# Whole loads of x, five fills ahead of the latents, and PSUM banks handed out by readiness, in a two-layer hybrid decoder trunk

## The chip, the cores and the metric

The kernel runs on one core of a Trainium2 chip. The metric is the device time of one execution in microseconds (us). In the rows below PE is the matrix engine (TensorE), DVE the vector engine, ACT the scalar engine, POOL GpSimd and SP the engine that here only issues DMAs. PEclk is the clock that TensorE was granted, 1.00 being the higher of its two levels (2.4 GHz) and 0.50 the lower (1.2 GHz).

## The reference

Two layers over x of 512 tokens by 1024 channels, float32. The part of a layer that the change touches:

```python
c_act = jax.nn.silu(c)
mod = c_act @ w_ada[l] + b_ada[l]
sh1, sc1, gt1, sh2, sc2, gt2 = [m[:, None, :] for m in jnp.split(mod, N_MOD, axis=-1)]
h = rms_norm(x, g_norm1[l]) * (1.0 + sc1) + sh1
u = h @ w_in[l] + b_in[l]
q_lat, kv_lat, k_rope, q_sb, k_sb, v_sb, gate_mla, gate_sb = jnp.split(u, IN_SPLIT_POINTS, axis=-1)
...
y_mla = causal_softmax_attention(q, k, v_mla)
y_sb = stick_breaking_attention(...)
merged = (jax.nn.sigmoid(gate_mla) * (y_mla @ w_branch_mla[l])
          + jax.nn.sigmoid(gate_sb) * (y_sb @ w_branch_sb[l]))
x = x + gt1 * (merged @ w_out[l])
```

q, k and the two latents are RMS-normed, and q and k get a rotary embedding from positions. A second norm and a gated MLP with a causal convolution of width 3 follow in each layer.

## The kernel before

Channels lie on the 128 partitions and the 512 tokens on the free axis, so x is eight tiles `xs[0..7]` of 128x512. Every float32 operand of a large product is split into a high and a low part, and one product is three matmuls (`mm3`): the high part of a weight is made by a cast on ACT or DVE (out of a buffer of the tag "raw", of which there are three), the low part by a subtraction on DVE.

The program is recorded as a list of operations. A list scheduler (`order`) then puts them into one order for each engine by estimated costs and by a priority, which is the place in the program plus `R.bias`; the lowest goes first, so that work with a bias of 400 stands back behind 400 later operations and slips into gaps. All engines' instructions therefore carry the one line that emits them, L1240 (L1235 for a table load of ACT). A buffer of the tag "ps", one of PSUM's eight banks, is granted in program order.

Layer 0 begins so. SP issues sixteen loads of 128x256, first the left halves of all eight tiles of x, then the right halves. ACT squares a half tile at a time, DVE adds the squares, and one matmul with a matrix of ones gives the sum over all channels of that half (`rsqrt_wide`). ACT issues four small loads of the positions and one of the rotary frequencies, between its squares. DVE works out rotary angles (`rope_tables`) on 128x512.

The modulation (sc1 and sh1, a column of 128 for each of the eight channel tiles k) is made in two ways. `ada_products` does it on PE: four loads of weights and 16 products of 128x1, which are 32 rows in the trace. `ada_tile` does it on DVE: two loads of 256 KB of `wada` and two multiply-and-sum instructions of 128x512 (CUSTOM_DVE in the rows). Before the change k = 0 and k = 1 take `ada_products`, k = 2 to 7 take `ada_tile`, two of them for each k.

The first projection of layer 0 fills eight banks, that is eight column blocks of 128 of w_in: four of the latents and the shared rotary key, four of the stick-breaking heads. It loops over k, and each k adds three matmuls to each bank, 24 matmuls in all. For k = 0 the work is in two halves of 256 tokens with seven banks; the eighth bank is done whole at k = 1. Then come `latents` (norms of the latents on ACT and DVE with small products in between), and a weave of the latent attention, the stick-breaking attention and *fills*: a fill is one more column block of the first projection, either a part of a stick-breaking head (`sb_proj`) or a gate (`gate`), 24 matmuls of 128x512 that need nothing but h and a weight. `FILLS` of them stand in the program ahead of the latents, at bias 400. `GATES` is how many of the 16 gates are fills at all; the others are done behind the attention. Layer 1 has the same shape, with seven banks.

Of the kernel before, what the change touches and what calls it, by code (L numbers as in the profile page):

```python
# [40 lines left out]
UNITS = 241  # L41
# [40 lines left out]
class Slot:  # L82
    def __init__(self, tag, dt, n):
        self.tag, self.dt, self.n = tag, dt, n
        self.mem = None
        self.log = []
        self.users = []
        self.index = 0
# [6 lines left out]
class Program:  # L95
# [3 lines left out]
    AFTER = {"pe": 200.0, "act": 145.0, "dve": 130.0, "pool": 160.0, "dma": 1050.0, "adma": 1050.0}  # L99
# [39 lines left out]
    def order(self):  # L139
# [8 lines left out]
        for o in self.ops:  # L148
            for t in o.slots:
                if t.users[0] is o or self.tags[t.tag]["bufs"]:  # L150
                    waiting.setdefault(t, []).append(o)
                    o.left += 1
# [14 lines left out]

        def release(o, time):
            o.left -= 1
            if o.left == 0:  # L170
                push(time, o)

        def grant(tg, time):
            while tg["next"] < len(tg["queue"]) and tg["used"] < tg["bufs"]:
# [26 lines left out]
        for o in self.ops:  # L201
            if o.left == 0:
                push(0.0, o)
        for tg in self.tags.values():
            grant(tg, 0.0)
        done = []
        while events:
# [6 lines left out]
            elif kind == "end":  # L214
# [7 lines left out]
                for q in o.succ:  # L222
                    lat = 0.0 if (q.eng == "pe" and o.eng == "pe") else self.AFTER[o.eng] + (80.0 if q.eng == "pe" else 0.0)
                    q.left -= 1
                    if q.left == 0:
                        push(time + lat, q)
            for name, e in engines.items():
# [82 lines left out]
FILLS = 2  # L310
EVERY = 4
GATES = 4
BIAS_E = 100
BIAS_R = 150
# [20 lines left out]
def trunk_kernel(ctx, tc, keys, xT, wstream, wada, cols, cvec, pos, freqs, out):  # L335
# [8 lines left out]
    def bank():  # L344
        return R.slot("ps")
# [64 lines left out]
    def dma(o, i, nbytes, writes=(), reads=(), eng="dma"):  # L410
        R.add(eng, "dma_start", max(nbytes / 360.0 + 10, 480.0), None, writes, reads, out=o, in_=i)
# [22 lines left out]
    HALF = (slice(0, S // 2), slice(S // 2, S))  # L434
    colt = [const(NCOL) for _ in range(DEPTH)]
    load(colt[0], cols[0], "adma")
    row = R.slot("raw", D)[0:1]
    load(row, cvec, "adma")
    xs = [slot() for _ in range(KC)]

    def load_x(n):
        for k in range(KC):
            load(xs[k][:, HALF[n]], xT[k][:, HALF[n]])

    load_x(0)
# [3 lines left out]
    act(row, row, AF.Silu)  # L449
# [11 lines left out]
    R.bias = BIAS_S  # L461
    for n in range(2):
# [4 lines left out]
        act(cact[:, c], ps, AF.Copy, alone=True)  # L467
    R.bias = 0
# [61 lines left out]
    def rsqrt_wide(sq, div, out=None):  # L530

        ps = bank()[:, 0:sq.n]
        mm(ps, ones, sq, True, True)
        r, q = (slot() if out is None else out)[:, 0:sq.n], slot()[:, 0:sq.n]
# [5 lines left out]
        return r  # L540
# [13 lines left out]


# [120 lines left out]
    def rope_tables():  # L676

        posv, freq = slot(dt=I32), slot()[:, 0:1]
        for i in range(4):
            load(posv[:, i * P:i * P + P], pos[32 * i:32 * i + 1].to_broadcast([P, P]), "adma")  # L680
        load(freq, freqs, "adma")
        sign = epsc[:, 3:4]
        for i in range(4):
            memset(sign[32 * i:32 * i + 32], -1.0 if i % 2 else 1.0)
        a, k = slot(), slot()
        R.add("dve", "tensor_copy", 330.0, None, [a], [posv], out=a, in_=posv)
# [13 lines left out]
        act(cosr, k, AF.Sin, scale=-1.0, bias=epsc[:, 2:3])  # L700
        act(sinr, a, AF.Sin, scale=sign)
# [276 lines left out]
    def layer(l, xs, xsrc, first, r=None, later=None):  # L978
# [3 lines left out]
        if l == 0:  # L982

            acc = [slot()[:, 0:S // 2] for _ in HALF]

            def start_norm(n):
                for k in range(KC):
                    x = xs[k][:, HALF[n]]
                    if k == 0:
                        act(acc[n], x, AF.Square)  # L990
                    else:
                        sq = slot()[:, 0:S // 2]
                        act(sq, x, AF.Square)
# [9 lines left out]
            load_x(1)  # L1003
            R.bias = BIAS_R
            rope_tables()
            R.bias = 0
# [328 lines left out]
```

## Time and profile before

| what | value |
|---|---|
| time, three runs | 1470.82 to 1473.1 us, median 1471.37 |
| the profiled execution | 1474.78 us, span 1473.0 us |
| mean granted clock of TensorE | 0.993 |
| busy: PE, DVE, ACT | 1445.1, 1029.7, 675.6 us |

The span runs from the first to the last instruction of the profiled execution; its time has 1.8 us more. A busy time sums what the trace counts as work on that engine; a matmul that runs at the lower clock, or drags, counts as busy all the same.

### The profile page before, as it was taken

The page shows a single profiled execution, that of the slowest core. Times are in us where ns is not written, and L with a number is a line of the kernel's source. Part 1 is how long each engine was busy: PE and PEld are TensorE (multiplying, and loading weights), DVE is VectorE, ACT ScalarE, POOL GpSimd, SP SyncE. Part 2 cuts the span into 40 slices and gives each one's busy share as a digit, 9 for nine tenths or more (in the row PEclk, how much of TensorE's full clock was granted, in tenths as well). Part 3 has the DMA queues.
Part 4 walks back from the last instruction along what each step waited for, and adds up shares of the span by engine and source line. Part 5 has one row for each costly group of instructions (what it writes and reads, how often), then busy time and mean ns, then how long its engine had stood idle before and what let it go on. Part 6 is the DMA issues. An engine that isn't in the chain of part 4 may idle for free.

```text
span 1473.0 us, 19263 instructions
## 1 busy us (share of the span) xinstructions
PE 1445.1 (98%) x7121; PEld 1218.4 (83%) x7121; DVE 1029.7 (70%) x2069; ACT 675.6 (46%) x1224; POOL 3.3 (0%) x18
## 2 busy tenths in 40 slices
PE   5999999999999999999999999999999999999998
PEld 4877888888988888888898788888889888888887
DVE  5888899956699987878364888944639675356641
ACT  4377876433444422334144787933416342233420
POOL 0000000000000000000000000000000000000000
PEclk9999999999999999999999999999999999999999
DMA  8421138755266676534230112433603333322311
GB/s 289 154 61 47 58 95 300 250 193 191 73 212 194 208 236 222 164 122 127 98 95 16 56 47 74 127 102 90 198 13 115 115 90 124 87 85 88 113 44 43
DMA packets 69792, 184.80 MB, mean 125 GB/s; under 512 B 7873, under 2 KB 11201, under 8 KB 69698
## 3 DMA queue, kind: packets, MB, share of 16 engines
q1 hardware_dynamic: 68832, 183.15, 39.2%
q8 instruction: 56, 0.92, 0.3%
q10 hardware_dynamic: 866, 0.41, 0.2%
q14 instruction: 38, 0.31, 0.1%
HBM read 179.34 MB, written 4.19 MB: 125 GB/s over the span
## 4 chain that ended last, share of the span: by engine, by line
PE 92%; ACT 3%; DVE 2%; DMA 1%; issue 0%; SPq 0%; DVEq 0%; ACTq 0%
PE ps L1240 92%; ACT s L1240 3%; DVE s L1240 2%; DMA s<-in_xT_dram 1%; DMA s<-in_wada_dram 0%; DMA s<-in_freqs_dram 0%; DMA raw<-in_wstream_dram 0%; DVE sm L1240 0%; SPq L1240 0%; ACT sm L1240 0%; DVEq L1323 0%; DVE c L1240 0%; DVEq L1240 0%; ACTq L1240 0%
## 5 line engine op out<-in xcount | busy, mean ns | idle before, releaser
L1240 PE MATMUL ps<-s,s 128*128 128x512 f32 (+2 forms) x6625 | 1413.2, 372 | 5.5 <-DVE s L1240 2.4
L1240 PEld LDWEIGHTS ps<-s,s 128*128 128x128 f32 x6625 | 1157.8, 190 | 220.0 <-DVE s L1240 6.9
L1240 ACT ACTIVATE s<-raw 128x512 fp32r<-128x512 f32 (+1 forms) x413 | 247.1, 622 | 364.5 <-PE ps L1240 207.9
L1240 DVE TENSOR_TENSOR s<-raw,s 128x512 fp32r<-128x512 f32 (+1 forms) x470 | 308.3, 682 | 151.1 <-PE ps L1240 86.3
L1240 ACT ACTIVATE s<-s 128x512 f32<-128x512 f32 (+7 forms) x372 | 210.9, 585 | 225.4 <-DVE s L1240 216.0
L1240 DVE SCALAR_TENSOR_TENSOR s<-ps,c,s 128x510 f32<-128x510 f32 (+4 forms) x249 | 175.3, 727 | 108.9 <-PE ps L1240 104.1
L1240 DVE TENSOR_TENSOR s<-s,s 128x512 fp32r<-128x512 f32 (+6 forms) x318 | 194.4, 621 | 31.7 <-ACT s L1240 23.9
L1240 ACT ACTIVATE s<-ps,c 128x512 f32<-128x512 f32 (+2 forms) x141 | 98.7, 721 | 80.4 <-PE ps L1240 80.1
L1240 DVE CUSTOM_DVE_ANT_0 s<-s,c,c 128x512 f32<-128x512 f32 x92 | 68.2, 747 | 15.1 <-DMA s<-in_wada_dram 15.0
L1240 DVE CUSTOM_DVE_ANT_0 s<-s,c,sm 128x512 f32<-128x512 f32 x92 | 68.3, 749 | 12.4 <-DMA s<-in_wada_dram 9.6
L1240 ACT ACTIVATE s<-ps 128x512 f32<-128x512 f32 (+3 forms) x118 | 63.5, 549 | 21.4 <-PE ps L1240 20.4
L1240 PE MATMUL ps<-c,s 128*128 128x1 f32 (+1 forms) x264 | 53.9, 264 | 3.2 <-DVE s L1240 2.4
L1240 PE MATMUL ps<-s,c 128*128 128x256 f32 (+3 forms) x140 | 48.3, 380 | 4.9 <-DVE s L1240 4.3
L1240 DVE TENSOR_SCALAR s<-ps,c 128x512 f32<-128x512 f32 (+1 forms) x33 | 25.9, 786 | 34.8 <-PE ps L1240 32.5
L1240 DVE TENSOR_SCALAR s<-raw 128x512 fp32r<-128x512 f32 (+1 forms) x57 | 23.7, 420 | 35.0 <-PE ps L1240 29.3
L1240 PEld LDWEIGHTS ps<-c,s 128*128 128x128 f32 x264 | 41.6, 193 | 7.0 <-DVE s L1240 3.9
L1240 ACT ACTIVATE s<-s,c 128x256 fp32r<-128x256 f32 (+1 forms) x56 | 27.5, 525 | 30.6 <-DVE s L1240 30.5
L1240 DVE SCALAR_TENSOR_TENSOR s<-s,c,s 128x256 fp32r<-128x256 f32 (+3 forms) x72 | 37.9, 554 | 0.6 <-ACT s L1240 0.4
L1240 PEld LDWEIGHTS ps<-s,c 128*128 128x128 f32 x140 | 26.3, 196 | 10.7 <-DVE s L1240 5.9
L1240 DVE TENSOR_TENSOR s<-ps,s 128x512 fp32r<-128x512 f32 (+1 forms) x40 | 25.0, 633 | 4.3 <-ACT s L1240 3.9
L1240 DVE TENSOR_TENSOR s<-s,ps 128x512 f32<-128x512 f32 x32 | 21.4, 683 | 6.4 <-PE ps L1240 6.4
L1240 DVE SCALAR_TENSOR_TENSOR s<-ps,s 128x512 f32<-128x512 f32 (+1 forms) x38 | 23.2, 614 | 2.5 <-ACT s L1240 2.2
(50 smaller groups left out, 251.9 us busy)
## 6 DMA issues: line engine op xcount, KB each, us to landing
raw<-in_wstream_dram SPq DMA_DIRECT2D x221, 512.0 KB, 3.7
s<-in_wada_dram SPq DMA_DIRECT2D x184, 256.0 KB, 4.0
raw<-in_wstream_dram SPq DMA_DIRECT2D x12, 448.0 KB, 3.4
s<-in_xT_dram SPq DMA_DIRECT2D x16, 128.0 KB, 4.0
s<-in_wstream_dram SPq DMA_DIRECT2D x8, 256.0 KB, 5.2
s<-in_xT_dram SPq DMA_DIRECT2D x8, 256.0 KB, 3.4
keep<-s SPq DMA_DIRECT2D x8, 256.0 KB, 2.7
s<-keep SPq DMA_DIRECT2D x8, 256.0 KB, 4.0
```

The lines of the kernel that those rows point to most:

```text
L1240: getattr(engines[o.eng], o.name)(**kw)
```

## The change

1. The start. x comes in eight whole loads of 128x512. Squares are whole, except that of the last tile, which is in halves, as are the two matmuls with ones and what follows from them. Positions and frequencies are loaded by SP behind x, as 128x128; ACT issues none of these loads. The rotary tables are worked out on 128x128, and 32 ACT copies of 32x128 spread them.
2. Only k = 0 takes `ada_products`; k = 1 is on DVE as the others. For k = 0 all eight banks are in halves.
3. `FILLS` goes from 2 to 5 and `GATES` from 4 to 8, in both layers.
4. The scheduler: a PSUM bank is granted when the first product into it could run, the most urgent first, and some of its costs are changed (the delay of a DMA 1050 to 2000).

```diff
-    AFTER = {"pe": 200.0, "act": 145.0, "dve": 130.0, "pool": 160.0, "dma": 1050.0, "adma": 1050.0}
+    AFTER = {"pe": 200.0, "act": 145.0, "dve": 130.0, "pool": 160.0, "dma": 2000.0, "adma": 2600.0}
...
+            elif wants(o):
+                heapq.heappush(wanting, (o.prio, o.seq, o))
+                banks(time)
+
+        def banks(time):
+            tg = self.tags["ps"]
+            while wanting and tg["used"] < tg["bufs"]:
+                o = heapq.heappop(wanting)[2]
+                t = next(t for t in o.slots if self.tags[t.tag]["psum"])
+                tg["used"] += 1
+                t.index = tg["free"].pop(0)
+                release(o, time)
...
-FILLS = 2
+FILLS = 5
 EVERY = 4
-GATES = 4
+GATES = 8
 BIAS_E = 100
-BIAS_R = 150
+BIAS_R = 250
+BIAS_T = 20
 BIAS_S = 60
 BIAS_A = 40
 BIAS_F = 400
...
     row = R.slot("raw", D)[0:1]
     load(row, cvec, "adma")
+    act(row, row, AF.Silu)
+    load(colt[0], cols[0], "adma")
     xs = [slot() for _ in range(KC)]
-
-    def load_x(n):
-        for k in range(KC):
-            load(xs[k][:, HALF[n]], xT[k][:, HALF[n]])
-
-    load_x(0)
+    for k in range(KC):
+        load(xs[k], xT[k])
+    posv, freq = slot(dt=I32)[:, :P], slot()[:, 0:1]
+    load(posv, pos)
+    load(freq, freqs)
     cact = const(D)
     ccol = const(KC)
     act(ccol, colt[0][:, C_C:C_C + KC], AF.Silu)
-    act(row, row, AF.Silu)
```

```diff
@@ -675,15 +706,8 @@
 
     def rope_tables():
 
-        posv, freq = slot(dt=I32), slot()[:, 0:1]
-        for i in range(4):
-            load(posv[:, i * P:i * P + P], pos[32 * i:32 * i + 1].to_broadcast([P, P]), "adma")
-        load(freq, freqs, "adma")
-        sign = epsc[:, 3:4]
-        for i in range(4):
-            memset(sign[32 * i:32 * i + 32], -1.0 if i % 2 else 1.0)
-        a, k = slot(), slot()
-        R.add("dve", "tensor_copy", 330.0, None, [a], [posv], out=a, in_=posv)
+        a, k = slot()[:, :P], slot()[:, :P]
+        R.add("dve", "tensor_copy", 130.0, None, [a], [posv], out=a, in_=posv)
         ts(a, a, freq, ALU.mult)
         two_pi = 2 * np.pi
...
         act(k, a, AF.Abs)
-        act(cosr, k, AF.Sin, scale=-1.0, bias=epsc[:, 2:3])
-        act(sinr, a, AF.Sin, scale=sign)
+        act(k, k, AF.Sin, scale=-1.0, bias=epsc[:, 2:3])
+        act(a, a, AF.Sin)
+        R.bias = BIAS_R
+        for q in range(4):
+            for o, t, f in ((cosr, k, 1.0), (sinr, a, -1.0 if q % 2 else 1.0)):
+                for i in range(4):
+                    act(o[32 * q:32 * q + 32, i * P:i * P + P], t[32 * i:32 * i + 32], AF.Copy, scale=f)
...
-            acc = [slot()[:, 0:S // 2] for _ in HALF]
-
-            def start_norm(n):
-                for k in range(KC):
-                    x = xs[k][:, HALF[n]]
-                    if k == 0:
-                        act(acc[n], x, AF.Square)
-                    else:
-                        sq = slot()[:, 0:S // 2]
-                        act(sq, x, AF.Square)
-                        tt(acc[n], acc[n], sq, ALU.add)
-                rsqrt_wide(acc[n], D, r[:, HALF[n]])
-
+            tot = [bank()[:, c] for c in HALF]
+            acc = slot()
+            for k in range(KC - 1):
+                square(acc, k, xs[k])
+            for c in HALF:
+                square(acc, KC - 1, xs[-1], c)
+            for n, c in enumerate(HALF):
+                mm(tot[n], ones, acc[:, c], True, True)
             r = slot()
-            start_norm(0)
+            for n, c in enumerate(HALF):
+                rsqrt_of(tot[n], D, r[:, c], slot()[:, c])
+            R.bias = BIAS_T
+            rope_tables()
             R.bias = BIAS_A
             ada_products(0, (8, 0))
             w = unit("first", l, 0, w=P * nb)
             R.bias = 0
-            load_x(1)
-            R.bias = BIAS_R
-            rope_tables()
-            R.bias = 0
-
-            banks = [bank() for _ in range(nb - 1)]
+
+            banks = [bank() for _ in range(nb)]
             h = [pair()]
-            for n in range(2):
-                if n:
-                    start_norm(1)
-                p = modulate(l, 0, 0, xs[0], r[:, HALF[n]], h[0], HALF[n])
-                for g in range(nb - 1):
-                    mm3(banks[g][:, HALF[n]], w, g, p, n == 0, False, True)
+            for n, c in enumerate(HALF):
+                p = modulate(l, 0, 0, xs[0], r[:, c], h[0], c)
+                for g in range(nb):
+                    mm3(banks[g][:, c], w, g, p, n == 0, False, True)
             for k in range(1, KC):
-                v = w
                 R.bias = BIAS_A
-                if k == 1:
-                    ada_products(0, (8 + k, k))
-                else:
-                    ada_tile(0, 8 + k)
-                    ada_tile(0, k)
+                ada_tile(0, 8 + k)
+                ada_tile(0, k)
                 w = unit("first", l, k, w=P * nb)
                 R.bias = 0
                 h.append(modulate(l, 0, k, xs[k], r, pair()))
-                if k == 1:
-                    banks.append(bank())
-                    mm3(banks[-1], v, nb - 1, h[0], True, False, True)
                 for g in range(nb):
                     mm3(banks[g], w, g, h[k], False, k == KC - 1, True)
```

At the start of PE's program stood, before the change (names are out<-weights or data; `c16_114` is silu(c) as columns, `s_8_105` and `s_9_153` the sums of squares of the two halves, `s_23_233` and `s_25_243` weights of the first projection, `s_31_255` the high part of the left half of h):

```order
L1240 MATMUL ps_2_176<-s_8_105,c1_76 128x256 [waits DVE_49]
L1240 MATMUL ps_3_195<-c16_114,s_19_180 128x1 [waits DMAHW7_49]
L1240 MATMUL ps_3_195<-c16_114,s_19_180 128x1 x3
L1240 MATMUL ps_3_195<-c16_114,s_20_185 128x1 [waits DMAHW0_49]
L1240 MATMUL ps_3_195<-c16_114,s_20_185 128x1 x3
L1240 MATMUL ps_3_195<-c16_114,s_21_192 128x1 [waits DMAHW1_49]
L1240 MATMUL ps_3_195<-c16_114,s_21_192 128x1 x3
L1240 MATMUL ps_3_195<-c16_114,s_22_198 128x1 [waits DMAHW2_49]
L1240 MATMUL ps_3_195<-c16_114,s_22_198 128x1 x3
L1240 MATMUL ps_3_238<-s_9_153,c1_76 128x256 [waits DVE_49]
L1240 MATMUL ps_4_261<-s_31_255,s_23_233 128x256 [waits Activation_49]
```

and now (`c15_107` is silu(c), `s_10_98` the sums of squares of all tokens):

```order
L1254 MATMUL ps_2_143<-c15_107,s_24_134 128x1 [waits DMAHW4_49,Activation_49]
L1254 MATMUL ps_2_143<-c15_107,s_24_134 128x1 x3
L1254 MATMUL ps_2_143<-c15_107,s_25_141 128x1 [waits DMAHW5_49]
L1254 MATMUL ps_2_143<-c15_107,s_25_141 128x1
L1254 MATMUL ps_3_168<-s_10_98,c1_76 128x256 [waits DVE_49]
L1254 MATMUL ps_4_172<-s_10_98,c1_76 128x256 [waits DVE_49]
L1254 MATMUL ps_2_143<-c15_107,s_25_141 128x1 x2
L1254 MATMUL ps_2_143<-c15_107,s_26_151 128x1 [waits DMAHW6_49]
L1254 MATMUL ps_2_143<-c15_107,s_26_151 128x1 x3
L1254 MATMUL ps_2_143<-c15_107,s_27_159 128x1 [waits DMAHW7_49]
L1254 MATMUL ps_2_143<-c15_107,s_27_159 128x1 x3
L1254 MATMUL ps_5_232<-s_32_226,s_28_206 128x256 [waits Activation_49]
```

The two matmuls with ones now stand next to each other inside the products of k = 0, and the 128x1 products of k = 1, which were further down in the rows before (from `ps_3_304<-c16_114,s_43_223 128x1 [waits DMAHW4_49]` on), are gone.

Around the latents of layer 0 PE's program had, before (`ps_3_930` and `ps_0_934` are heads of the latent attention, `s_12_745` and `s_44_757` their weights):

```order
L1240 MATMUL ps_6_835<-s_42_699,s_78_694 128x512
L1240 MATMUL ps_6_835<-s_23_704,s_78_694 128x512
L1240 MATMUL ps_3_930<-s_89_921,s_12_745 128x512 [waits Activation_49]
L1240 MATMUL ps_0_934<-s_89_921,s_12_745 128x512
L1240 MATMUL ps_6_835<-s_42_699,s_77_734 128x512
L1240 MATMUL ps_3_930<-s_88_932,s_12_745 128x512 [waits DVE_49]
L1240 MATMUL ps_2_943<-s_81_936,s_27_747 128x512 [waits PE_49,Activation_49]
L1240 MATMUL ps_3_930<-s_89_921,s_44_757 128x512
L1240 MATMUL ps_0_934<-s_88_932,s_12_745 128x512
L1240 MATMUL ps_3_930<-s_71_927,s_12_745 128x512
L1240 MATMUL ps_0_934<-s_89_921,s_44_757 128x512
L1240 MATMUL ps_2_943<-s_35_947,s_27_747 128x512 [waits DVE_49]
```

and now (`ps_6_851`, `ps_7_937` and `ps_0_960` are fills; `ps_5_950` is the latent attention's first projection):

```order
L1254 MATMUL ps_7_937<-s_32_226,s_62_761 128x512
L1254 MATMUL ps_6_851<-s_36_697,s_54_710 128x512
L1254 MATMUL ps_7_937<-s_33_238,s_62_761 128x512
L1254 MATMUL ps_6_851<-s_38_712,s_54_710 128x512
L1254 MATMUL ps_5_950<-s_87_927,s_35_902 128x512 [waits Activation_49]
L1254 MATMUL ps_6_851<-s_36_697,s_69_733 128x512
L1254 MATMUL ps_5_950<-s_39_941,s_35_902 128x512 [waits DVE_49]
L1254 MATMUL ps_7_937<-s_32_226,s_63_822 128x512
L1254 MATMUL ps_0_960<-s_32_226,s_82_858 128x512
L1254 MATMUL ps_7_937<-s_44_340,s_62_761 128x512
L1254 MATMUL ps_0_960<-s_33_238,s_82_858 128x512
L1254 MATMUL ps_7_937<-s_45_358,s_62_761 128x512
```

Where products of the latents stood next to each other, rows of fills now stand between them.

On ACT, late in the attention of layer 0, there stood before (an `ACTIVATE` with three names on the right is an exponential of the attention that also sums):

```order
L1240 ACTIVATE s_19_2245<-s_27_2108 128x512 [waits DVE_49]
L1235 ACT_TABLE_LOAD
L1240 ACTIVATE s_88_2223<-s_88_2223 128x512 [waits Activation_49]
L1235 ACT_TABLE_LOAD
L1240 ACTIVATE s_77_2247,sm_5_2248<-s_77_2247,sm_5_2248,sm_31_1937 128x128 [waits DVE_49]
L1240 ACTIVATE s_54_2295<-ps_3_2060 128x256 [waits PE_49]
L1240 ACTIVATE s_46_2289,sm_6_2290<-s_46_2289,sm_6_2290,sm_31_1937 128x256 [waits DVE_49]
L1240 ACTIVATE s_48_2316<-raw_2_2131 128x512 [waits DMAHW1_49,PE_49]
L1240 ACTIVATE s_41_2325<-ps_7_2210,c8_96 128x512 [waits PE_49]
```

and now:

```order
L1254 ACTIVATE s_1_1994<-raw_1_1893 128x512 [waits DMAHW4_49,PE_49]
L1254 ACTIVATE s_13_2000<-ps_1_1982 128x512 [waits PE_49]
L1254 ACTIVATE s_49_2021<-ps_2_1913,c7_90 128x512 [waits PE_49]
L1254 ACTIVATE s_62_2027<-ps_3_2002 128x512 [waits DVE_49]
L1254 ACTIVATE s_63_2031<-ps_1_2023,c2_78 128x512 [waits PE_49]
L1254 ACTIVATE s_63_2031<-s_63_2031 128x512 [waits Activation_49]
L1249 ACT_TABLE_LOAD
```

```order
L1254 ACTIVATE s_40_2096<-s_57_2086 128x512 [waits Activation_49]
L1254 ACTIVATE s_41_2110<-raw_0_1920 128x512 [waits DMAHW5_49,PE_49]
L1254 ACTIVATE s_69_2101,sm_4_2102<-s_69_2101,sm_4_2102,sm_26_1721 128x256 [waits DVE_49]
L1254 ACTIVATE s_8_2124<-ps_6_1783 128x512 [waits PE_49]
L1254 ACTIVATE s_48_2130<-s_8_2124 128x512 [waits Activation_49]
```

Over the whole program ACT's table loads go from 19 to 27: in each layer the group of five at this place becomes nine, since gates stand between the exponentials as fills.

The engines' instruction counts otherwise move little: PE 7019 to 7006, DVE 2071 to 2049, ACT 1201 to 1251 (32 of them the copies of 32x128, eight the table loads, 13 more casts of raw weights), SP 480 to 474.

## Rows read from the trace of the kernel before

**Rows 1.** The page: busy time (share) and count; then the chain that ended last.
```profile
PE 1445.1 (98%) x7121; PEld 1218.4 (83%) x7121; DVE 1029.7 (70%) x2069; ACT 675.6 (46%) x1224; POOL 3.3 (0%) x18
PE 92%; ACT 3%; DVE 2%; DMA 1%; issue 0%; SPq 0%; DVEq 0%; ACTq 0%
```

**Rows 2.** Waits of PE, whole span: us in total, times, longest.
```profile
PE ps L1240 <- ACT raw L1240: 10.2, 1, 10.2
PE ps L1240 <- DVE s L1240: 9.0, 9, 3.7
```

**Rows 3.** Timeline of PE, 9 to 44 us: start, us, what, count, [idle before].
```profile
10.25 3.75 PE L1240 MATMUL ps<-raw,c 1*128 1x512 f32 x4 [10.25 <-ACT raw L1240]
17.70 1.22 PE L1240 MATMUL ps<-s,c 128*128 128x256 f32 x2 [3.71 <-DVE s L1240]
18.71 6.83 PE L1240 MATMUL ps<-c,s 128*128 128x1 f32 x32
28.49 4.64 PE L1240 MATMUL ps<-s,s 128*128 128x256 f32 x20 [1.41 <-ACT s L1240]
...
39.24 2.29 PE L1240 MATMUL ps<-c,s 128*128 128x1 f32 x20
41.84 2.47 PE L1240 MATMUL ps<-s,s 128*128 128x512 f32 x4 [0.32 <-DVE c L1240]
```

**Rows 4.** The chain that ended last, 0 to 60 us: start, us, what.
```profile
10.63 4.23 DMA s<-in_freqs_dram
```

**Rows 5.** Timeline of SP and of ACT, 0 to 14 us.
```profile
0.80 9.96 SPq L1240 DMA_DIRECT2D s<-in_xT_dram  x16
11.01 1.95 ACT L1240 ACTIVATE s<-s 128x256 f32<-128x256 f32 x6 [0.91 <-DMA s<-in_xT_dram]
```

**Rows 6.** Timeline of DVE, 14 to 21 us.
```profile
14.95 0.48 DVE L1240 TENSOR_SCALAR s<-s,s 128x512 f32<-128x512 f32 x1 [1.49 <-DMA s<-in_freqs_dram]
...
16.70 3.40 DVE L1240 TENSOR_TENSOR s<-s,s 128x256 f32<-128x256 f32 x7
```

**Rows 7.** Windows: PE, PEld, DVE, ACT, POOL busy (count), PEclk, DMA share, GB/s.
```profile
20.00:30.00 10.00, 8.27 (x35) 7.47 (x36) 7.56 (x21) 3.26 (x8) 0.00 (x0) 1.00 1.02 366
40.00:50.00 10.00, 9.65 (x36) 7.40 (x36) 8.37 (x22) 3.99 (x7) 0.56 (x3) 0.66 0.31 95
50.00:60.00 10.00, 10.00 (x46) 8.29 (x45) 9.93 (x26) 3.02 (x6) 0.00 (x0) 1.00 0.84 288
100.00:110.00 10.00, 8.57 (x44) 7.34 (x43) 9.30 (x18) 9.79 (x19) 0.00 (x0) 0.82 0.17 52
110.00:120.00 10.00, 8.95 (x38) 6.13 (x37) 9.66 (x22) 9.88 (x22) 0.00 (x0) 0.84 0.00 0
200.00:300.00 100.00, 100.00 (x475) 83.44 (x474) 90.59 (x213) 61.03 (x108) 0.00 (x0) 1.00 0.71 238
500.00:600.00 100.00, 100.00 (x443) 82.84 (x442) 83.69 (x177) 31.61 (x53) 0.00 (x0) 1.00 0.69 222
810.00:820.00 10.00, 9.35 (x51) 7.17 (x50) 9.54 (x20) 9.70 (x20) 0.00 (x0) 1.00 0.00 0
820.00:830.00 10.00, 7.98 (x35) 5.20 (x34) 9.25 (x19) 9.51 (x21) 0.00 (x0) 0.83 0.18 52
830.00:840.00 10.00, 10.00 (x44) 8.68 (x43) 7.76 (x30) 5.73 (x15) 0.00 (x0) 0.83 0.15 48
```

**Rows 8.** Timeline of PE, 75 to 100 us: what follows the first loop.
```profile
83.98 1.91 PE L1240 MATMUL ps<-s,c 128*128 128x512 f32 x4
```

**Rows 9.** Timeline of PE, 100 to 120 us: a wait in the latents.
```profile
105.85 1.00 PE L1240 MATMUL ps<-c,s 128*128 128x1 f32 x6 [1.43 <-DVE s L1240]
```

**Rows 10.** DVE's groups by form, 50 to 70 us.
```profile
L1240 DVE CUSTOM_DVE_ANT_0 s<-s,c,c 128x512 f32<-128x512 f32 x8 | 5.8, 748 | 0.0
```

**Rows 11.** Timeline of ACT, 87 to 91 us: a table load.
```profile
88.49 1.28 ACT L1235 ACT_TABLE_LOAD   x1
89.79 1.26 ACT L1240 ACTIVATE s<-ps,c 128x512 f32<-128x512 f32 x2
```

More of the change, by code (lines that the diff above doesn't have):

```diff
@@ L39 @@
 NCOL = C_C + KC
-UNITS = 241
+UNITS = 239
 NAMES = ("xT", "wstream", "wada", "cols", "cvec", "pos", "freqs")
@@ L87, in __init__ @@
         self.users = []
-        self.index = 0
+        self.index = -1
 class Op:
@@ L149, in order @@
             for t in o.slots:
-                if t.users[0] is o or self.tags[t.tag]["bufs"]:
+                if t.users[0] is o or not self.tags[t.tag]["psum"]:
                     waiting.setdefault(t, []).append(o)
@@ L166, in push, with wants @@
             heapq.heappush(events, (when, seq, "ready", o))
+        wanting = []
+        def wants(o):
+            return o.left == 1 and any(self.tags[t.tag]["psum"] and t.users[0] is o and t.mem is None and t.index < 0 for t in o.slots)
         def release(o, time):
@@ L171, in release @@
                 push(time, o)
+            elif wants(o):
[9 more added lines that the diff above has]
+                release(o, time)
         def grant(tg, time):
+            if tg["psum"]:
+                banks(time)
+                return
             while tg["next"] < len(tg["queue"]) and tg["used"] < tg["bufs"]:
@@ L203, in order @@
                 push(0.0, o)
+            elif wants(o):
+                heapq.heappush(wanting, (o.prio, o.seq, o))
         for tg in self.tags.values():
@@ L226, in order @@
                         push(time + lat, q)
+                    elif wants(q):
+                        heapq.heappush(wanting, (q.prio, q.seq, q))
+                        banks(time)
             for name, e in engines.items():
@@ L410, in dma @@
     def dma(o, i, nbytes, writes=(), reads=(), eng="dma"):
-        R.add(eng, "dma_start", max(nbytes / 360.0 + 10, 480.0), None, writes, reads, out=o, in_=i)
+        R.add(eng, "dma_start", max(nbytes / 360.0 + 10, 480.0) if eng == "dma" else 420.0, None, writes, reads, out=o, in_=i)
     def load(v, src, eng="dma"):
@@ L433, in trunk_kernel @@
     cosr, sinr = const(S), const(S)
-    HALF = (slice(0, S // 2), slice(S // 2, S))
     colt = [const(NCOL) for _ in range(DEPTH)]
-    load(colt[0], cols[0], "adma")
     row = R.slot("raw", D)[0:1]
     load(row, cvec, "adma")
+    act(row, row, AF.Silu)
+    load(colt[0], cols[0], "adma")
     xs = [slot() for _ in range(KC)]
-    def load_x(n):
-        for k in range(KC):
-            load(xs[k][:, HALF[n]], xT[k][:, HALF[n]])
-    load_x(0)
+    for k in range(KC):
[3 more added lines that the diff above has]
+    load(freq, freqs)
     cact = const(D)
@@ L459, in trunk_kernel @@
     mods = [const(64) for _ in range(DEPTH)]
-    R.bias = BIAS_S
     for n in range(2):
@@ L466, in trunk_kernel @@
         mm(ps, ones[0:1], row[:, c], True, True)
-        act(cact[:, c], ps, AF.Copy, alone=True)
-    R.bias = 0
+        R.bias = BIAS_S
+        act(cact[:, c], ps, AF.Copy)
+        R.bias = 0
     def make_masks():
@@ L528, in norm, with rsqrt_wide, rsqrt_of @@
         return across(rsqrt_cols(acc, D, 0))
-    def rsqrt_wide(sq, div, out=None):
-        ps = bank()[:, 0:sq.n]
+    def rsqrt_wide(sq, div):
+        ps = bank()
         mm(ps, ones, sq, True, True)
-        r, q = (slot() if out is None else out)[:, 0:sq.n], slot()[:, 0:sq.n]
+        r = slot()
+        rsqrt_of(ps, div, r, slot())
+        return r
+    def rsqrt_of(ps, div, r, q):
         act(r, ps, AF.Ln, scale=1.0 / div, bias=epsc[:, 0:1])
@@ L539, in rsqrt_wide @@
         stt(r, q, 1.5, r, ALU.add, ALU.mult)
-        return r
     def modulate(l, i, k, x, r, h, c=slice(0, S)):
@@ L553, in pair @@
         return slot(dt=F32R), slot(dt=F32R)
+    HALF = (slice(0, S // 2), slice(S // 2, S))
     def residual(xs, tiles, prods, gate, acc):
```

1 line of the change is left out of this document (removed).

## The prediction

> **What bounds the kernel now.** I read the page first. PE is busy for 1445.1 of 1473.0 us, and the chain of work that ended last runs 92% over PE, with ACT at 3% and DVE at 2% [rows 1]. So only what takes time off PE, or fills a gap on it, can move the end. In the undisturbed middle of the program PE does 443 matmuls in 100 us at full clock [rows 7], that is 0.226 us for a matmul of 128x512, and a fill or one k of the first loop (24 of them) takes 5.42 us. That is work no edit here removes. What can be saved lies where PE does less, and three places show in the list of PE's waits, its timeline and the windows.
>
> The first is the start. PE's waits put 10.2 us on the scalar engine's raw row and 9.0 on DVE's results [rows 2]. The first dense matmul of the first projection runs at 28.49 [rows 3]. The steps ahead of it: the chain hangs on the load of the rotary frequencies, issued at 10.63 and landing 4.23 later [rows 4], because DVE's angle work waits for it at 14.95 and the seven adds of the squares stand behind it in DVE's queue, to 20 [rows 6]. The matmul with ones runs at 17.70. Right behind it stand 32 rows of 128x1 products, 6.83 us, and the dense work needs their columns [rows 3]. The dense matmuls then take 0.23 us each for 256 columns (20 in 4.64), twice what full clock gives.
>
> The second place is just behind: the products for k = 1, of which 20 rows take 2.29 us from 39.24, a wait of 0.32, and a granted clock of 0.66 for 40 to 50 us [rows 3, 7]: 3.4 us lost at the lower level of 1.2 GHz. Before the fall PE did little but 128x1 products and that wait. The first loop ends at 83.98 [rows 8].
>
> The third place is the latents, once in each layer. From 100 to 120 us PE idles 1.43 + 1.05 us and the clock is 0.82 and 0.84, which is 3.4 us more: 5.9 in all. From 810 to 840 it idles 0.65 + 2.02, and the clock is 0.83 twice: 6.1 in all [rows 7]. What it waits for is DVE (1.43 at 105.85 [rows 9]), with ACT busy at 95 to 99% and DVE at 93 to 97% [rows 7]. In the two stretches of 100 us taken from elsewhere PE stands at 100%.
>
> **The change, part by part.**
>
> *The start.* Sixteen issues took SP 9.96 us [rows 5]; eight whole loads are 2.1 MB, at the 366 GB/s of 20 to 30 us [rows 7] some 5.7 us of transfer, with a latency of about 4 (as the 4.23 of rows 4) in front: I estimate the last tile at 9.3 to 10. Squares go at 1.95/6 = 0.33 us a half [rows 5], adds at 3.40/7 = 0.49 [rows 6], and the frequencies, now behind x, no longer hold up the adds except the very last, since the angle work stands among them in DVE's order. So the two sums may run at about 11.7. PE's order has six products first, then both sums, then the other ten products. The products' weights are loaded behind x and should land from about 10.8. From there PE has 32 rows at 0.213 (6.83/32) and two sums at 0.9 (17.70 to 18.71 was 1.0 for one), 8.6 us in all, to 19.4. The columns, h's left half and its cast take about 1.6 more: DVE's two column steps, one multiply-add, one cast, at 0.2 to 0.5 each. First dense matmul at 21.0 in place of 28.49: **-7.5**. The bounds are -5.5 (weights 2 us later) and -8.5 (the products done in a shorter time).
>
> *k = 1 on DVE.* PE loses 32 rows of 128x1, by 2.29/20 each: **-3.7**. The eighth bank's k = 0 goes from three matmuls of 512 at full clock to six of 256 at 0.23: **+0.7**. The fall of the clock at 41.5 had 128x1 products and a wait ahead of it, both now gone, so I take it as gone: **-3.4**, and the wait **-0.3**; the other bound is 0, if the clock falls elsewhere in the loop. What covers the four new instructions on DVE is the slow k = 0 phase on PE, 48 matmuls and about 10 us. Without that cover they are 4 x 0.73 = 2.9 us (5.8/8 each [rows 10]).
>
> Sum of the start: -14.2; the loop then ends near 69.8.
>
> *Fills ahead of the latents.* Three more fills are 16 us of PE work that needs neither DVE's norms nor ACT's, and it comes out of the attention, where PE stands at 100% with or without it [rows 7]. In the order they lie one by one between the rows that waited. They bring casts and low parts to ACT and DVE, already at 93 to 99% there, so the latents' chain itself gets longer; PE is covered for 16 us, against 5.9 us of loss in layer 0 and 6.1 in layer 1. The lower bound of the gain is nothing (the waits come back behind the fills). The upper is the 12.0 of both, and an estimated 3 more for what PE drags there without a recorded wait (six 128x1 rows in 1.00 us at 105.85 [rows 9], 0.17 each, against 2.29/20 = 0.11): 15 us. I take **-5** and **-5.5**, nearly all of the recorded loss less a wait of a microsecond where the first scores of the stick-breaking need their splits.
>
> *Gates as fills.* Eight more table loads on ACT. A load is 1.28 us, and from its start at 88.49 to the next instruction at 89.79 it costs 1.30 [rows 11]: 8 x 1.30 = 10.4 us of ACT. In 200 to 300 us, where five loads lie, ACT is busy at 61% and PE at 100% [rows 7], so most of it is hidden; without the cover all 10.4 would show. I take **+1.5** (bounds 0 and 10.4). The Trainium skill (ScalarE: Activation LUTs, section "What ACT_TABLE_LOAD costs") says that a switch costs a drain of about 1.38 us beside the load's 1.28, 2.66 together. By that ACT would lose 21 us and my term would double. The trace shows no such drain at 88.49.
>
> *The scheduler.* PSUM's grant and the costs change the order alone; their price is in the waits above. 32 small ACT copies and the rotary work are behind the start, under dense PE work: 0.
>
> Sum: -14.2 - 5 - 5.5 + 1.5 = -23.2. On the profiled execution's own 1474.8 us that is 1451.6. Its median of three runs is 3.4 us lower, so **1448 us**.
>
> **The rivals.**
>
> *Only the start gains.* DVE and ACT are full in the latents [rows 7]; if the fills' own splits push the norms out by as much as the fills cover, the waits only move. Against it: 16 us of cover. Then -14.2 + 1.5: 1458.7.
>
> *The latents lose their drag too.* PE's pace under the lower clock and with late operands goes as well, -15 instead of -10.5, and the k = 0 phase runs faster: 1442.
>
> *The first loop becomes DVE's.* DVE is at 9.93 of 10 us in 50 to 60 with PE at 100% [rows 7]; k takes it about 5.0 to 5.5 us against PE's 5.42. With k = 1 added and no slack from a slow clock, 0.5 us a k are 3.5 us, with a fall of the clock (3.4) 6.9: 1451.5 to 1455.
>
> *The start gains little.* The sum now needs all of x and not half. If x comes 5 us later than I think, the sum runs near 17 as before and the products are done ahead of it: first dense about 23, and 1450; with the weights behind x late as well, 1455.
>
> *Slower.* The table loads sit on the attention's chain of exponentials. They decide from 24.7/8 = 3.1 us of PE each. A load that stops PE for 1.3 us and brings a stretch of low clock that loses as the one at 41.5 did (3.4) costs 4.7: 38 us over eight, 1484. Against it are the five loads of 200 to 300 us, with PE at 100%.
>
> **How the numbers follow.** My sum has a chance of 0.5 (1444 to 1453 alone), only the start 0.16, the loop or the start short 0.17, the drag gone too 0.1. Slower by over 0.2% (3 us, about what a measurement of this kernel can tell) has 0.04, no change 0.03. The range from 1440 to 1459 leaves out about 2 in 10.
>
> **What would show it.** In the profile of the changed kernel: the first 128x256 of dense work near 21; one group of 32 rows of 128x1 there and no more; no window with a clock under 0.9 up to 70; the loop's last product near 70; the windows with the lowered clock around 90 to 130 and 780 to 830 gone, or PE idle under 1 us in them; nine table loads in each attention beside a PE at 100%. It would be wrong if PE shows new waits for ACT in the attention, for DVE in the loop, or at the products of the stick-breaking, above all with a clock that falls there.

## The result, and the profile after

The changed kernel takes 1452.42 us (median of four runs, 1451.93 to 1452.79) against 1471.09 us before: 18.7 us less, a ratio of 0.987 with a 95% interval of 0.9853 to 0.9887. The profiled executions lie further apart, 1473.0 against 1451.1 us of span, 21.9 us; the profiled execution of the kernel before (1474.78 us) was slower than all four runs that its median is taken from.

The page of the changed kernel, which answers to [rows 1]: busy time with share and count, then the shares of the chain that ended last.

```profile
PE 1432.3 (99%) x7092; PEld 1207.1 (83%) x7092; DVE 1020.2 (70%) x2047; ACT 706.8 (49%) x1279; POOL 3.2 (0%) x14
...
PE 90%; DVE 4%; ACT 4%; DMA 2%; issue 1%; DVEq 0%; SPq 0%; ACTq 0%
```

PE's busy time has fallen by 12.8 us, though only 29 rows have gone: matmuls that ran at the lower clock before count for most of it. The mean granted clock went from 0.993 to 1.000, which over 1473 us is 10.3 us, nearly half of the difference between the two profiles. In the trace of the changed kernel the clock is recorded at the lower level only from 1450.08 us on, in the last microsecond.

The waits of PE over the whole span, as in [rows 2] (us in total, times, longest), and its timeline up to 46 us, as in [rows 3]:

```profile
PE ps L1254 <- ACT c L1254: 5.4, 1, 5.4
PE ps L1254 <- ACT s L1254: 3.6, 5, 1.7
PE ps L1254 <- DVE s L1254: 2.9, 7, 0.7
PE ps L1254 <- DMA s<-in_wstream_dram: 2.0, 1, 2.0
```

```profile
11.18 2.69 PE L1254 MATMUL ps<-c,s 128*128 128x1 f32 x12 [2.05 <-DMA s<-in_wstream_dram]
13.72 2.05 PE L1254 MATMUL ps<-s,c 128*128 128x256 f32 x4
15.57 4.27 PE L1254 MATMUL ps<-c,s 128*128 128x1 f32 x20
21.55 14.01 PE L1254 MATMUL ps<-s,s 128*128 128x256 f32 x72 [1.71 <-ACT s L1254]
36.27 9.92 PE L1254 MATMUL ps<-s,s 128*128 128x512 f32 x41 [0.72 <-ACT s L1254]
```

The first dense matmul starts at 21.55 in place of 28.49. The group that follows is 48 of 256 columns and 24 of 512, named by its first shape. The latents' first sum with ones starts at 69.83, where it was 83.98 [rows 8].

The record of the clock begins late. Its first value stands at 26.72 us in this trace and at 38.10 in that of the kernel before; ahead of it the windows show 1.00 because nothing is recorded. There PE's own pace has to tell the level. The timeline of the changed kernel, cut at 26.7 us (what spans the cut stands in both parts):

```profile
21.55 5.40 PE L1254 MATMUL ps<-s,s 128*128 128x256 f32 x24 [1.71 <-ACT s L1254]
...
26.41 3.57 PE L1254 MATMUL ps<-s,s 128*128 128x256 f32 x26
```

Up to there one matmul of 256 columns follows another after 0.21 us, behind it after 0.12. PE thus began at about half its later pace, before as after, and the 1.00 of 20 to 30 us in [rows 7] is no reading of its clock. The dense work runs so from 28.49 to 38.1 before, 9.6 us, and from 21.55 to 26.7 now, 5.2 us.

Windows of the changed kernel around the latents, with the columns of [rows 7]:

```profile
100.00:110.00 10.00, 9.32 (x45) 6.73 (x43) 8.82 (x19) 9.06 (x20) 0.00 (x0) 1.00 0.00 0
110.00:120.00 10.00, 9.96 (x57) 8.76 (x56) 9.62 (x31) 6.77 (x17) 0.00 (x0) 1.00 0.24 59
...
200.00:300.00 100.00, 99.94 (x472) 83.27 (x471) 95.09 (x221) 57.46 (x104) 0.00 (x0) 1.00 0.73 240
...
820.00:830.00 10.00, 9.35 (x52) 7.65 (x51) 9.77 (x23) 9.90 (x22) 0.00 (x0) 1.00 0.00 0
```

Where the clock was 0.82, 0.84 and 0.83 it is 1.00, and PE idles 0.7 us in 100 to 120 in place of 2.5.

To put all kernels on one scale I took from each trace, for each matmul, the time to the start of the next one less the usual pitch of its form (0.2266 us for 512 columns, 0.12 for 256, 0.112 for the 128x1 products, the form's median for the rest), and summed it over stretches. This counts waits, low clock and drag alike. The first column is the start of PE's first matmul; the others are stretches in us of the span. The cut at 84 lies behind the first loop of the kernel before; those at 130 and 850 lie behind the last stretch of low clock that any of these kernels has in the latents. The cuts are the same for all, so each kernel is cut at a slightly different place of its program, and a few tenths between two cells say nothing.

```
kernel       first   to 84  84-130  130-300  300-780  780-850  from 850
before        10.2    18.9    10.2     11.1      2.6     11.8      10.5
after          5.4    14.5     4.4     12.4      2.8      7.3      10.9
s_start        5.2    14.5    11.5      8.8      2.1     12.0       9.5
a_f2g4         5.3    14.1    12.6     10.6      2.4     13.5      11.2
a_banks        5.2    14.7     5.1     10.4      2.6      5.8       9.9
s_oldplan      4.1    15.1     4.7     10.5      3.1      5.8       9.8
b_f5g8        10.2    17.2     5.4     11.0      2.5      5.9      10.5
b_banks       10.2    16.3    14.8     11.0      2.4     14.8      11.6
```

Before to after: the start gives 4.8 + 4.4 and an estimated 3.7 of removed products (32 rows at 2.29/20), the latents 5.8 and 4.5, and the attention of layer 0 takes back 1.3.

### The profile page after: what moved, and what is told of

Its sections match the earlier page's. It is cut to its first block, busy times and chain, and to the rows that moved or that the text cites. A ratio compares the mean times of both kernels' runs of the same rounds, so it can differ in the third digit from the quotient of the medians.

```text
span 1451.1 us, 19263 instructions
## 1 busy us (share of the span) xinstructions
PE 1432.3 (99%) x7092; PEld 1207.1 (83%) x7092; DVE 1020.2 (70%) x2047; ACT 706.8 (49%) x1279; POOL 3.2 (0%) x14
## 4 chain that ended last, share of the span: by engine, by line
PE 90%; DVE 4%; ACT 4%; DMA 2%; issue 1%; DVEq 0%; SPq 0%; ACTq 0%
PE ps L1254 90%; DVE s L1254 4%; ACT s L1254 3%; DMA raw<-in_wstream_dram 1%; DMA s<-in_xT_dram 1%; ACT c L1254 1%; DMA s<-in_wada_dram 0%; ACT L1249 0%; DVE c L1254 0%; DVE sm L1254 0%; ACT sm L1254 0%; DVEq L1254 0%; SPq L1254 0%; ACTq L1254 0%
## 5 line engine op out<-in xcount | busy, mean ns | idle before, releaser
L1254 ACT ACTIVATE s<-raw 128x512 fp32r<-128x512 f32 (+1 forms) x428 | 257.0, 622 | 324.7 <-PE ps L1254 215.2
L1254 DVE TENSOR_TENSOR s<-raw,s 128x512 fp32r<-128x512 f32 x470 | 307.6, 682 | 132.7 <-PE ps L1254 59.7
L1254 DVE TENSOR_TENSOR s<-s,s 128x512 fp32r<-128x512 f32 (+7 forms) x312 | 194.6, 629 | 33.8 <-ACT s L1254 25.4
L1254 ACT ACTIVATE s<-ps,c 128x512 f32<-128x512 f32 (+2 forms) x146 | 105.2, 728 | 98.2 <-PE ps L1254 98.0
L1254 ACT ACTIVATE s<-ps 128x512 f32<-128x512 f32 (+3 forms) x120 | 64.0, 550 | 24.2 <-PE ps L1254 22.8
L1254 PE MATMUL ps<-s,c 128*128 128x512 f32 (+3 forms) x140 | 46.8, 372 | 1.6 <-DVE s L1254 1.1
L1254 DVE TENSOR_SCALAR s<-raw 128x512 fp32r<-128x512 f32 (+1 forms) x42 | 17.6, 422 | 37.9 <-PE ps L1254 33.8
L1254 ACT ACTIVATE s<-s,c 128x256 fp32r<-128x256 f32 (+2 forms) x58 | 28.8, 527 | 31.3 <-DVE s L1254 27.0
L1254 DVE SCALAR_TENSOR_TENSOR s<-s,c,s 128x256 fp32r<-128x256 f32 (+2 forms) x72 | 37.9, 553 | 2.4 <-ACT s L1254 2.2
L1254 DVE TENSOR_SCALAR s<-ps,c 128x512 f32<-128x512 f32 (+1 forms) x28 | 21.5, 769 | 23.2 <-PE ps L1254 17.4
L1254 DVE SCALAR_TENSOR_TENSOR s<-ps,s 128x512 f32<-128x512 f32 (+1 forms) x38 | 23.1, 617 | 10.4 <-ACT s L1254 9.7
```

What stands on the lines that cost most here:

```text
L1254: getattr(engines[o.eng], o.name)(**kw)
```

## The experiments

The theory: the start is worth some 14 us, the fills some 8 to 10, table loads and scheduler next to nothing. The rivals: it is all the start; the table loads cost; the grant of banks is what makes the fills work. The experiments ran in three groups on their own chips, each beside the kernel before (median 1475.38, 1472.1 and 1472.39). The kernel before scatters: its runs in the three groups go from 1469.4 to 1478.6 us with mean clocks of 0.991 to 0.995. The changed kernel's eight runs lie between 1451.9 and 1454.2, so I compare times of the kernels near a clock of 1.00 with each other too.

**Without the fills.** FILLS and GATES as before, or FILLS alone.

```diff
-FILLS = 5
+FILLS = 2
-GATES = 8
+GATES = 4
```

> The changed kernel with two fills ahead of the latents and four gates as fills, as before the change; the start and the scheduler stay as changed. Theory (the start is worth some 14 us, the fills some 8, the table loads cost 1 to 2): about 1459 us, with PE idle for over 1.5 us in each of the two latents and a stretch of granted clock near 0.83 back in them, and a first loop that ends near 70 as in the changed kernel. Rival (the fills move nothing in the end, it is all the start and the scheduler): 1452 to 1454.

> The changed kernel with FILLS 2 in place of 5, GATES stays 8, so the nine table loads in each attention stay. Theory: the waits of the latents come back, 1460 to 1461 us, 1 to 2 us above the kernel that has four gates too. Rival: 1452 to 1454, since the waits lie elsewhere.

Measured: 1465.01 us, ratio 0.9931 (0.9912 to 0.995), and with FILLS alone undone 1465.37, ratio 0.9936 (0.9918 to 0.9955). Both miss on the high side of the theory and refute the rival: the fills are worth 11 to 13 us here, not 8 (11.2 against the kernel with FILLS 5 and GATES 4 that follows, on the same chip). A window of the first:

```profile
90.00:100.00 10.00, 6.26 (x23) 4.68 (x23) 7.66 (x16) 7.98 (x15) 0.00 (x0) 0.63 0.02 7
```

With two fills in place of five, PE is idle for 3.7 of these 10 us and the clock falls to 0.63. The latents lose 12.6 and 13.5 us in the table, more than the 10.2 and 11.8 of the kernel before. The new start is the smaller part of the reason: `s_start` below, which has it too but grants banks in program order, loses 11.5 and 12.0, so that 2.6 of the 4.1 us go with the grant.

The edit did to the table loads what the expectation did not foresee. With FILLS 2 and GATES 8 the trace counts three in each attention, not nine.

**Only the gates.** GATES 4, FILLS 5.

> The changed kernel with GATES 4 in place of 8, FILLS stays 5: no more than five table loads in each attention. Theory (the loads are hidden under a busy PE): 1450 to 1452 us, 0 to 1.5 less than the changed kernel. First rival (each of the eight loads costs PE its 1.3 us): 1442. Second rival (the four more gates are what keeps PE fed in the attention once three fills have gone ahead): slower, 1455 or more, with new waits of PE between 120 and 300 us.

Measured: 1453.81 us, ratio 0.9859 (0.9838 to 0.9879), clock 0.999. Beside the changed kernel's 1452.42 and (in the next group) 1453.78 this is no gain, and PE is not starved by the missing gates either. On the table loads it says nothing, because the edit did not take them away. The trace has 27, nine in each attention, as the changed kernel has; the groups of ACT in 120 to 300 us are the same in both:

```profile
L1249 ACT ACT_TABLE_LOAD x9 | 11.5, 1283 | 0.2
```

So the four more gates as fills are not what makes five loads nine, as I had it when I described the change.

**Only the fills, on the kernel before.**

```diff
-FILLS = 2
+FILLS = 5
-GATES = 4
+GATES = 8
```

> The kernel before with FILLS 5 and GATES 8, nothing else of the change. Theory (fills are worth the same without the new start): 1463 to 1465 us, with the low-clock stretches in the latents gone and the one at 41 to 48 us kept. Rival (with banks granted in program order the fills hold banks that the latents wait for, so that they gain nothing): 1470 or slower.

Measured: 1460.55 us, ratio 0.9904 (0.9886 to 0.9921), 14.8 less than the kernel before on its chip; more than expected. That chip's median for the kernel before is the highest of the three; against the 1472.1 and 1472.39 of the others it would be 11.6 to 11.8. The latents' windows are whole, and the low stretch at 41 to 48 stays:

```profile
40.00:50.00 10.00, 9.31 (x28) 7.09 (x29) 9.93 (x23) 5.23 (x9) 0.00 (x0) 0.66 0.48 155
...
110.00:120.00 10.00, 9.97 (x54) 8.03 (x53) 9.07 (x20) 9.73 (x22) 0.00 (x0) 1.00 0.00 0
```

Two constants give over half of all that the change gives, and the old grant of banks doesn't keep them from it. They bring the table loads too, nine in layer 0's attention for five and seven in layer 1's for five, and yet PE loses 11.0 us in 130 to 300 against 11.1.

**The changed kernel again**, for the group that follows.

> The changed kernel once more, beside the three that follow. Its time against the kernel before should be as it was (ratio 0.985 to 0.989) and its granted clock 1.00 with no lowered stretch after the start.

Measured: 1453.78 us, ratio 0.988 (0.9866 to 0.9895), as before. The clock was 0.999: one stretch at the lower level, 157 to 161 us, which the first profile didn't have, so it is no fixed part of the change. PE's waits around it are the same in both profiles, 0.4 us once between 145 and 165 us.

**k = 1 on PE again.**

```diff
-                ada_tile(0, 8 + k)
-                ada_tile(0, k)
+                if k == 1:
+                    ada_products(0, (8 + k, k))
+                else:
+                    ada_tile(0, 8 + k)
+                    ada_tile(0, k)
```

> The changed kernel with the modulation of k = 1 on PE again (32 rows of 128x1). Theory (the lowered clock at 41 to 48 us of the kernel before came from these products): the products cost 3.7 us and a lowered stretch of 6.8 us comes back between 30 and 50 us, 3.4 more: 6 to 8 us above the changed kernel. Rival (the products alone): 3 to 4 us above, with a granted clock of 1.00 throughout. Second rival (the first loop is bound by DVE, which now has less to do): 0 to 2 above.

Measured: 1454.76 us, ratio 0.9889 (0.9872 to 0.9905): 1.0 above the changed kernel beside it. My theory's 6 to 8 fall, and so do the first rival's 3 to 4; the second rival's size fits. Against the 1452.42 of the first result it is 2.3, so 1.0 to 2.3 is what can be said. PE's timeline:

```profile
14.96 9.81 PE L1257 MATMUL ps<-c,s 128*128 128x1 f32 x46
24.63 1.84 PE L1257 MATMUL ps<-s,s 128*128 128x256 f32 x7
...
28.90 17.38 PE L1257 MATMUL ps<-s,s 128*128 128x256 f32 x84
```

The products do stand ahead of the dense work, which starts at 24.63 in place of 20.86. No fall of the clock is recorded behind them. But they all run at the slow pace of the beginning, 0.21 us a row, which lasts to 32.78 us here, where the clock's record begins, in place of 24.25. There was no higher level to fall from, so the run does not test what the theory says of the clock. What it costs, the longer slow pace included, is set against the waits for ACT of 1.71 and 0.69 us, which are gone.

The first loop hangs on different engines in the two kernels. The chain that ended last, from 30 to 72 us, first with k = 1 on PE and then as changed:

```profile
by line: PE ps L1257 100.6%
```

```profile
by line: DVE s L1254 53.5%; PE ps L1254 17.6%; issue 11.1%; ACT c L1254 10.3%; ACT s L1254 4.2%; DVE c L1254 2.7%; DVE sm L1254 0.9%
```

In the changed kernel PE is busy for 10.00 of 10 us in 40 to 50 and in 50 to 60, and DVE for 9.96 and 9.93: k = 1 on DVE relieves PE, and the loop then hangs on DVE. With k = 1 on PE the first sum of the latents starts 4.0 us later (73.09 for 69.12), and 1.0 to 2.3 of that is left at the end. That ACT and DVE get ahead meanwhile, so that the latents lose less (3.7 against 4.5 us in 84 to 130), is a likely reason; it was not tested.

**x in sixteen halves**, all else as changed.

```diff
+    for n in (slice(0, S // 2), slice(S // 2, S)):
+        for k in range(KC):
+            load(xs[k][:, n], xT[k][:, n])
-    for k in range(KC):
-        load(xs[k], xT[k])
```

> The changed kernel with x loaded in sixteen halves (all left halves, then all right halves), everything else as changed, so that squares of whole tiles wait for both. Theory (eight more issues of 0.4 to 0.5 us on SP stand ahead of the products' weights, and PE waits for these): the first dense matmul 3 to 4.5 us later, 1 to 4 us above the changed kernel. Rival (transfers, not issues, set when the weights come): within 0.5 us.

Measured: 1455.17 us, ratio 0.9892 (0.9878 to 0.9907), 1.4 above the changed kernel beside it (2.8 above the first result), and the first dense matmul at 24.30 against 20.86, 3.4 later, both as the theory had it. PE waits for the products' weights behind x:

```profile
13.86 3.54 PE L1255 MATMUL ps<-c,s 128*128 128x1 f32 x16 [6.23 <-DMA s<-in_wstream_dram]
```

Again only a part of a delay ahead of the dense work is left at the end.

**Banks in program order**, in the changed kernel.

```diff
-                if t.users[0] is o or not self.tags[t.tag]["psum"]:
+                if t.users[0] is o or self.tags[t.tag]["bufs"]:
...
-            if tg["psum"]:
-                banks(time)
-                return
```

> The changed kernel with PSUM banks granted in program order, as before the change; the scheduler's costs stay changed. Theory (the grant by readiness gives little by itself): within 3 us of the changed kernel. Rival (the fills slip between the latents only because a bank goes to whoever can run): 8 us or more above it, with the waits and a lowered clock back in the latents of both layers.

Measured: 1449.44 us (1449.13 to 1449.87), ratio 0.9853 (0.9838 to 0.9868). It is 4.3 us faster than the changed kernel on the same chip (1453.78, lowest 1452.32), and 3.0 faster than the 1452.42 of the first result. Neither theory nor rival had it: the part of the change that I had priced at nothing costs. In the table the changed kernel loses 2.0 more in the attention of layer 0 (12.4 against 10.4), 1.5 in the latents of layer 1 and 1.0 behind them; in the latents of layer 0 it is 0.7 better. The windows of 120 to 300 us, first of the changed kernel, then of this one:

```profile
120.00:300.00 180.00, 178.10 (x897) 148.92 (x896) 158.19 (x368) 123.51 (x231) 0.00 (x0) 1.00 0.49 157
```

```profile
120.00:300.00 180.00, 179.14 (x904) 150.63 (x904) 159.52 (x375) 123.80 (x232) 0.00 (x0) 1.00 0.49 162
```

1.0 us of the 2.0 is idle time of PE that shows; the rest is matmuls that follow each other late without a recorded wait.

**The grant by readiness alone, on the kernel before**: the four pieces that the change adds to `order`, its costs left as they were.

> The kernel before with the grant of banks by readiness alone. Theory (the grant costs some 2 us in each attention, whatever stands ahead of it): 3 to 6 us slower than the kernel before. Rival (it costs only where more fills compete for banks): within 1.5 us of the kernel before.

Measured: 1479.13 us, ratio 1.004 (1.0025 to 1.0056): 6.7 us slower by the medians, a little more than the theory's 3 to 6. The theory of a cost holds, its place does not. The loss is in the latents, 14.8 and 14.8 us in the table against 10.2 and 11.8. In the attention of layer 0 there is none (11.0 against 11.1), behind the latents of layer 1 it is 1.1, and the start is 2.6 better. Windows of the latents:

```profile
100.00:110.00 10.00, 6.71 (x27) 4.53 (x27) 8.31 (x17) 7.97 (x16) 0.00 (x0) 0.83 0.06 23
...
820.00:830.00 10.00, 7.74 (x33) 6.30 (x31) 7.54 (x17) 6.91 (x14) 0.00 (x0) 0.72 0.19 52
```

Its window of 40 to 50 us has a clock of 1.00. The products of k = 1 are on PE here too, but all but eight rows run by 31.4 us, ahead of the first recorded clock at 35.97.

**Only the start.** FILLS 2, GATES 4, banks in program order.

> The change without its fills and without its grant of banks: FILLS 2, GATES 4, banks in program order; the start, k = 1 on DVE and the scheduler's costs as changed. Theory (the start is worth 14 us, and the grant costs some 4, which hid it when the fills alone were undone): 1457 to 1459 us on a chip where the kernel before takes 1472, 13 to 15 less than that one. Rival (the grant costs only in company with the fills, and the new start is worth 10): 1461 to 1464.

Measured: 1459.8 us, ratio 0.9913 (0.9898 to 0.9928), 12.6 less than the kernel before; between theory and rival, nearer the theory, and 5 less than with the grant by readiness (1465.01, another chip).

**The whole scheduler as before**, start and fills as changed.

```diff
-    AFTER = {... "dma": 2000.0, "adma": 2600.0}
+    AFTER = {... "dma": 1050.0, "adma": 1050.0}
```

> The changed kernel with the whole scheduler as before (banks in program order, DMA delays 1050, ACT's DMAs at the old cost). Theory (the costs give nothing beside the grant): 1448 to 1451 us, as the kernel with the old grant alone. Rival (the longer DMA delay lets PE's order avoid waits at the start): 1453 or more, with waits of PE for DMA or for late splits before 70 us.

Measured: 1449.61 us (1448.95 to 1450.71), ratio 0.9845 (0.9828 to 0.9861), the same as with the grant alone undone (1449.44), so the costs give nothing. It is 22.8 us below the kernel before on its chip, and these two are the fastest that were run.

**Fewer gates with banks in program order.**

> The changed kernel with banks in program order and GATES 4, so five table loads in each attention and not nine. Theory (the eight loads are hidden): 1449 to 1450.5 us, as with GATES 8. Rival (each costs a part of its 1.3 us once nothing else holds PE up): 1442 to 1447, the fastest of all.

Measured: 1451.13 us, ratio 0.9852 (0.9838 to 0.9867), 1.5 to 1.7 above the kernels with GATES 8. Again the edit took no table loads away: the trace has nine in each attention, where `a_banks` has nine and seven and `s_oldplan` seven and seven. Neither theory nor rival is tested by it, and whether the 1.5 us are a price of loads, of the gates or of another order is open.

## Why the prediction came out as it did

The time, 1452.4, lies in the range and just inside the likeliest case's own (1444 to 1453). The direction and most terms held, but the gain is 18.7 us and the sum had 23.2.

*The step that failed* is "The scheduler. ... the order alone; their price is in the waits above". The grant by readiness has a price of its own, 3.0 to 4.3 us in the changed kernel and 6.7 in the kernel before. The sum without it comes out: -23.2 predicted for everything else, -22.8 measured with the scheduler put back. In part that is luck, for the start gave less than its term and the fills more. I had looked at the order at the start and in the latents, not along the attention of layer 0 and through layer 1, where in the changed kernel the price is paid. Why an order made by readiness is the worse one there was not tried, nor whether another order by the same rule would cost as much; that the two orders made by it are worse is shown.

*The start*, -14.2, measured -12.6 by itself. First dense matmul: 21.0 predicted, 21.55 in the profile. Loop's end: 69.8 predicted, 69.83. Its inner terms are less sure than the sum. The -3.4 for the clock at 41 to 48 was tied to the products of k = 1 and a wait. The stretch went in every kernel with the new start, as forecast. The wait can't be the reason: in the kernel before the fall is recorded at 41.51, where the wait only begins. The products can: in the two profiles with the stretch, `before` and `b_f5g8`, 20 rows of them run at the full pace just ahead of it. In `a_k1pe` and `b_banks`, which have products and no stretch, all of them or all but eight run earlier, at the slow pace of the beginning. No run set this up on purpose, so the cause stays open. And k = 1 on DVE, -3.7 + 0.7 as counted, is worth 1.0 to 2.3, about what the start fell short by, since the loop's chain then runs over DVE. That is the rival "The first loop becomes DVE's", come true in the chain while PE stays busy. The slow phase of k = 0, taken as 48 matmuls and about 10 us of cover, was 5.2 us: from 26.7 on PE ran at its full pace.

*The fills*, -5 and -5.5. With the start and the old grant they are worth 10.2 to 10.4 us (1459.8 to 1449.61 and 1449.44), against 10.5 - 1.5. In the table (`s_start` to `a_banks`) the latents gain 6.4 and 6.2, and the attention of layer 0 gives 1.6 back. The rival "only the start gains" is refuted. On the kernel before the fills gave 14.8 (11.8 against the median of the kernel before in the third group), where 15 was the upper bound. Alone the parts gave -12.6 and -14.8, together -22.8. With the 11.8 they add up to within 1.6 us, less than the kernel before scatters by. The clock gains from both: 0.993 before, 0.996 with the start, 0.998 with the fills, 1.000 with both, in the profiled executions.

*The table loads*, +1.5, were not measured by themselves. Both runs that were to take eight loads away kept nine in each attention of their traces. What the traces do show: in 120 to 300 us of the changed kernel, with nine loads of 1.28 us, PE idles 1.9 us in all, and every wait recorded there is for DVE. With the new start the step from five loads to nine (`s_start` to `a_banks`) goes with 1.6 us more loss in the attention of layer 0 and 0.4 behind the latents of layer 1, and with the old start (`before` to `b_f5g8`) with none. So the term's size is possible, and the 10.4 us of loads without cover are excluded. The Trainium skill (ScalarE: Activation LUTs, section "What ACT_TABLE_LOAD costs") gives 2.66 us for a switch, with a drain in it. The trace shows no such drain here either; the next activation starts 1.29 us behind the load's start:

```profile
210.10 1.28 ACT L1249 ACT_TABLE_LOAD   x1
211.39 0.63 ACT L1254 ACTIVATE s<-s 128x512 f32<-128x512 f32 x1
```

*The own time and the median.* I took the 3.4 us between the profiled execution before and its median as a constant. It is scatter: that kernel's runs go from 1469.4 to 1478.6 us over all groups, the changed one's from 1451.9 to 1454.2. The clock is a part of it, but runs of the kernel before with the same mean clock, 0.994, go from 1469.7 to 1475.7. Against medians the sum still comes to -23.2, so this moved nothing but the difference between the profiles, 21.9, and that of the times, 18.7.

## What to carry to other kernels

Where PE idles a little between small products, count the lower clock that comes with it: two constants that put independent work between them gave 12 to 15 us, while PE's idle time in the latents before was 5 us by the windows. A change to a scheduler is a term of its own and wants a look along the whole order, not only at the places that it was made for; each of the parts should be run alone before they are put together. Whether an edit did what it was to do is read from the trace: GATES was to take eight table loads away here and left them as they were. A delay of 3 to 4 us ahead of the dense work came out as 1 to 3 us at the end, so a term at the start is priced by what feeds the dense work behind it.

## What the runs showed of the hardware

Three things were not expected. The low clock at 41 to 48 us stands in the two kernels where 20 rows of 128x1 products run at full pace for 2.3 us just ahead of it (39.24 to 41.53, the fall at 41.51, in the kernel before), and not where the products run in the slow beginning; the wait of 0.32 us there starts with the fall and not ahead of it. A stretch of 3.4 us at the lower level came up at 157 us in one execution of the changed kernel and not in another with the same waits, so a single profile's clock carries some 2 us of chance. And every profile begins without a recorded clock, to 24.25 us at the earliest and 38.10 at the latest, with PE at 0.21 us for a 128x1 row or a matmul of 256 columns where it later takes 0.11 and 0.12; a 1.00 in a window there must not be taken for the clock.
